# Expert strips issued as one set, and a pair's first output emitted ahead of its second gate product

## The chip, the cores and the metric

The kernel runs on one core of one Trainium2 chip. The metric is the device time of one execution in microseconds (us); the median of several runs is quoted. TensorE is called PE below, VectorE DVE, ScalarE ACT, GpSimd POOL and SyncE SP.

## What is computed

Two transformer blocks run one after the other on 256 tokens of width 1024, in fp32. The first block has two layers, each a token mixer and then a mixture of experts; the second has an attention layer, an RWKV layer and a plain MLP after each. The change touches the mixture of experts alone. Cut to that part, the reference computes, for each of 64 experts `e` and the tokens routed to it (8 experts for each token):

```
def run_block(args):
    e, toks, ws = args
    xb = x_pad[toks]
    hb = jax.nn.silu(xb @ w_gate[e]) * (xb @ w_up[e])
    return (hb @ w_down[e]) * ws[:, None]
...
routed = jax.ops.segment_sum(yb.reshape(P, D), tok_buf, num_segments=T + 1)[:T]
```

`w_gate` and `w_up` are 1024 x 256 for each expert, `w_down` is 256 x 1024. All 64 experts are used in both layers, so a layer loads 64 x 3 MB of expert weights.

## The kernel before, in words

**Groups, pairs, strips.** In `moe` (from L515) the experts are ranked by how many tokens they have, and by rank get room for 128 (4 experts), 64 (28) or 32 tokens (32). 256 such rows make a group, so there are 13 groups in a layer, in the order of `ORDER` (L33). A group is two pairs of 128 rows each (the code's `p_`, 0 and 1; called *units* here). A unit holds `k` experts side by side: 1, 2 or 4, each with a *strip* of 128, 64 or 32 columns of PE's stationary operand, and so of the 128 output partitions. A strip is one matmul of one expert's rows against 512 columns of that expert's weights. Strips of different experts of one unit stand in different column groups of the PE array.

**A unit's steps.** `up` (L842) makes the gate and up products: for each of 8 slices of the contraction, one strip for each expert, into the PSUM tile `gu`. The first four slices read the first half of the experts' weights, the last four the second half, and each half of each expert is a tile of its own. ACT then takes the silu (`hs`, L862), DVE the product (`hm`, L864). `down` (L870) transposes `hm` on PE (`hp`), ACT copies that to `hTe` (L878), and PE makes two outputs of 512 columns (`yps`), each with two slices of the contraction and one strip for each expert; ACT and DVE take them out as a high and a low part (`yH` L887, `yL` L888). `scatter` (L892) adds a group's rows to the tokens (`sca`). `pick` (L798) gathers the tokens of the next group ahead (`gat`, 4 steps of 16 matmuls).

**Loads.** `fetch` (L690) issues a unit's loads on SP: for each expert the first halves (gate and up, 512 KB each, into one 1 MB tile), the second halves, and then `dn` (1 MB): 3, 6 or 12 tiles a unit. All go through one pool of seven 1 MB buffers. A load waits until PE has read the tile that had its buffer.

**Side work.** Between these steps `side_work` (L734, L742) emits pieces of the second block's context path (attention and MLP beside the first mixture, RWKV beside the second), with two weight buffers of their own.

**What sets the order.** The program is traced once; then a scheduler puts each engine's instructions into a fixed order, by the order in which they were written and by when its own model of time finds an instruction's inputs ready. On the chip each engine runs its list in order, and an instruction that waits holds up all behind it. So a strip whose weights are modelled as loaded could be put on PE's list alone, long before the other strips of the same slice: `up` traced the strips one by one, and nothing held them together. `issue_after(x)` puts the instructions traced in its block behind `x` on x's engine.

Of the kernel before, what the change touches and what calls it, by code (L numbers as in the profile page):

```python
# [21 lines left out]
P = 128  # L22
D = 1024
KT = 8
# [14 lines left out]
def dap(ap, off, dims):  # L39
    return bass.AP(tensor=ap.tensor, offset=ap.offset + off, ap=[list(d) for d in dims])  # L40


class Net:
# [471 lines left out]
    def moe(self, l, x, row, mc, mce, rw, rb):  # L515
# [6 lines left out]
        hT = pp.tile([P, KT, S], F32, name="hT")  # L522
# [160 lines left out]
        wk = wks.enter_context(self.pool(name=f"mwk{l}", bufs=2))  # L683
        posT, wHL = self.tables(self.pos, self.wt, NE, mp)
# [5 lines left out]
        def fetch(q, pr):  # L690

            r0, w = groups[q]
            k = P // w
            with tc.issue_after(behind.pop(0)) if len(behind) > 1 else ExitStack():
                rvs = [nc.values_load(self.ei[0:1, r0 + pr * k + u:r0 + pr * k + u + 1],
                                      engines=[mybir.EngineType.SP], min_val=0, max_val=NE - 1) for u in range(k)]
            src = lambda n, u, j: i[n][l, bass.DynSlice(rvs[u], 1)].rearrange("e (p j) f -> p (e j) f", j=j)
            gus = [[self.wtile([2, 4, 256], [((v,), src(n, u, KT)[:, 4 * a:4 * a + 4, :])
                                             for v, n in enumerate(("w_gate", "w_up"))], "gu")
                    for u in range(k)] for a in range(2)]  # L700
            dn = [self.wtile([2, D], [(None, src("w_down", u, 2))], "dn") for u in range(k)]
            behind.append(self.load.ins)
            return gus, dn, False
# [3 lines left out]
        def start(q):  # L707
            r0, w = groups[q]
            sl = slice(r0, r0 + GROUP // w)
            return self.pick(self.pos[:, :, sl], r0, wHL[:, :, sl, :], mce, wk, w)  # L710

        g = drain_last(start(0))
        for q in range(nq):
            bg = BG_GROUP[groups[q][1]]
            if q == nq - 1:
                for t in range(2):
                    r = self.racc[:, t, :]
                    nc.vector.tensor_tensor(r, r, g2, op=OP.mult)
                    r = r.rearrange("q (p j) -> q j p", j=KT)
                    for v in xLH:  # L720
                        nc.vector.scalar_tensor_tensor(r, v[:, t], ALPHA, r, op0=OP.mult, op1=OP.add)
                gb = mp.tile([P, 2, D], F32, tag="xL", name="gb")
                for n, a in enumerate(("ln2_g", "ln2_b")):
                    nc.gpsimd.dma_start(gb[:, n], dap(i[a], l * D, [[0, P], [1, D]]))
            w = [fetch(q, 0)]
            h = [self.up(g, 0, posT, w[0], wk)]
            nxt = start(q + 1) if q + 1 < nq else iter(())
            n = next(nxt, None)
            w.append(fetch(q, 1))
            h.append(self.up(g, 1, posT, w[1], wk))  # L730
            self.down(g, 0, *h[0], w[0][1], wk)
            for _ in range(2):
                next(nxt, None)
            self.side_work(bg / 2)  # L734
            self.down(g, 1, *h[1], w[1][1], wk)
            for _ in nxt:
                pass
            if q < nq - 1:
                self.scatter(g)
            else:  # L740
                self.scatter(g, g2, wk)
            self.side_work(bg / 2)  # L742
            g = n
# [54 lines left out]
    def pick(self, pos, b0, wHL, mce, wk, w=SLOT):  # L798
# [40 lines left out]
        nc.vector.reduce_sum(wsl, wps.rearrange("p a b c -> p a (b c)"), axis=AX.X)  # L839
        yield g  # L840

    def up(self, g, p_, posT, weights, wk, nb=2):  # L842

        nc = self.nc
        gus, dn, wild = weights
        w = g["w"]
        k = P // w
        gu = self.acc([P, 512], "gu")
        sx = lambda j, u: g["xes"][j // 2][:, j % 2, (k * p_ + u) * w:(k * p_ + u + 1) * w]
        for j in range(KT):  # L850
            for v in range(2 if wild else 1):
                for u in range(k):
                    if wild:
                        self.mm(gu[w * u:w * u + w, 256 * v:256 * v + 256], sx(j, u), gus[v][u][:, j, :],
                                j == 0 and v == 0, j == KT - 1)
                    else:
                        self.mm(gu[w * u:w * u + w, :].rearrange("p (a b) -> p a b", a=2), sx(j, u),
                                gus[j // 4][u][:, :, j % 4, :], j == 0, j == KT - 1)
        bp = self.tr([P, S], "bp")
        self.mm(bp, g["eb"][:, P * p_:P * p_ + P], posT, True, True)  # L860
        hs = wk.tile([P, 256], F32, tag="hs", name="hs")
        nc.scalar.activation(hs, gu[:, :256], AF.Silu)  # L862
        hm = wk.tile([P, 2, P], F32, tag="hm", name="hm")
        nc.vector.tensor_tensor(hm.rearrange("q j p -> q p j"), hs.rearrange("q (p j) -> q p j", j=2),  # L864
                                gu[:, 256:].rearrange("q (p j) -> q p j", j=2), op=OP.mult)
        ohT = wk.tile([P, S], F32R, tag="ohT", name="ohT", bufs=nb + 1)
        nc.vector.tensor_scalar(ohT, bp, self.slotp[w], None, op0=OP.is_equal)
        return hm, ohT

    def down(self, g, p_, hm, ohT, dn, wk, nb=2):  # L870

        nc = self.nc
        hp = self.tr([P, 2, P], "hp")
        for j in range(2):
            self.transpose(hp[:, j, :], hm[:, j, :])
        w = g["w"]
        hT = wk.tile([P, 2, P], F32, tag="hT", name="hTe")
        nc.scalar.copy(hT, hp)  # L878
        yH = wk.tile([P, D], F32R, tag="yH", name="yH", bufs=nb)
        yL = wk.tile([P, D], F32R, tag="yL", name="yL", bufs=nb)  # L880
        for hf in range(2):
            sl = slice(hf * 512, hf * 512 + 512)
            y = self.acc([P, 512], "yps")
            for j in range(2):
                for u in range(P // w):
                    self.mm(y[w * u:w * u + w, :], hT[:, j, w * u:w * u + w], dn[u][:, j, sl], j == 0, j == 1)
            nc.scalar.activation(yH[:, sl], y, AF.Copy, scale=g["wsl"][:, p_:p_ + 1])  # L887
            nc.vector.scalar_tensor_tensor(yL[:, sl], y, g["wsl"][:, p_:p_ + 1], yH[:, sl], op0=OP.mult,  # L888
                                           op1=OP.subtract)
        g["ys"].append((ohT, yH, yL))  # L890
# [931 lines left out]
def drain_last(gen):  # L1822
    for v in gen:
        pass
    return v
# [114 lines left out]
```

## Time and profile before

| | |
|---|---|
| median of 3 runs | 3206.11 us (3203.72 to 3206.66) |
| the profiled execution's own time | 3199.65 us |
| its span, first to last instruction | 3197.9 us |
| granted TensorE clock, mean over the span | 0.925 of full speed |
| PE / DVE / ACT / POOL busy | 89% / 53% / 38% / 14% |
| mean over the span, moved by DMA | 234 GB/s |

The mixture of experts runs from about 350 to 1135 us (layer 0) and from about 1455 to 2135 us (layer 1) of the span: 1465 us in all. An fp32 matmul stands in the trace as two records, so a strip is "x2"; the trace shows 2048 records of `gu` and 1024 of `yps`, that is 1024 and 512 strips. Busy time is the time in which at least one record of a group runs, so strips that run side by side count once.

### The profile page before, as it was taken

How to read it: one execution, taken by the hardware profiler on the slowest of the kernel's cores; microseconds unless marked ns; L12 is line 12 of the kernel's file. 1: busy time of each engine (PE TensorE's matmuls, PEld its weight loads, DVE VectorE, ACT ScalarE, POOL GpSimd, SP SyncE). 2: the span in 40 equal slices, each digit the busy share in tenths (PEclk: the TensorE clock that was granted, in tenths of full speed). 3: DMA queues.
4: the chain of work that ended last, by engine and by line, in shares of the span. 5: the costliest groups of instructions: out<-in, count | busy, mean ns of one | idle time of the engine just before them, and what ended most of it. 6: DMA issues, size and time to landing. Idle time of an engine off the chain costs nothing.

```text
span 3197.9 us, 52845 instructions
## 1 busy us (share of the span) xinstructions
PE 2857.3 (89%) x20518; PEld 1879.6 (59%) x20518; DVE 1703.9 (53%) x3348; ACT 1224.0 (38%) x2237; POOL 450.4 (14%) x653
## 2 busy tenths in 40 slices
PE   5998988978999999999888989779999997878899
PEld 2776533544565568785444434345678785656698
DVE  3556433433344466663433434258876775565576
ACT  2553333322223246531323223224554445454443
POOL 1102000000000000100010010003023204343032
PEclk9999988989999999999999999889999997567899
DMA  9764798999988787636888888875345541002552
GB/s 334 280 220 161 268 349 316 347 355 349 401 299 323 257 298 269 218 125 248 313 323 306 336 320 321 320 264 181 104 126 172 171 129 25 11 8 67 176 189 80
DMA packets 237407, 748.25 MB, mean 234 GB/s; under 512 B 24288, under 2 KB 39560, under 8 KB 208480
## 3 DMA queue, kind: packets, MB, share of 16 engines
q1 hardware_dynamic: 230896, 728.56, 63.0%
q0 software_dynamic: 5920, 15.19, 1.6%
q8 instruction: 165, 2.70, 0.3%
q10 hardware_dynamic: 336, 1.06, 0.1%
q14 instruction: 90, 0.74, 0.1%
HBM read 738.56 MB, written 6.18 MB: 233 GB/s over the span
## 4 chain that ended last, share of the span: by engine, by line
PE 67%; DVE 9%; DMA 5%; ACT 5%; issue 3%; SPq 1%; POOL 0%; DVEq 0%; ACTq 0%; POOLq 0%
PE gu L76 12%; PE mu L76 9%; PE yps L76 7%; PE w L76 7%; PE gat L76 3%; PE sca L76 3%; DMA gu<-in_w_up_dram 2%; PE rk L76 2%; PE pg L76 2%; PE adaps L76 2%; DVE wl L240 1%; DMA w<-in_mlp_w_dram 1%; PE ao L76 1%; PE zy L76 1%; PE rv L76 1%
## 5 line engine op out<-in xcount | busy, mean ns | idle before, releaser
L240 DVE TENSOR_TENSOR wl<-w,wh 128x1024 fp32r<-128x1024 f32 (+1 forms) x432 | 472.9, 1101 | 322.1 <-ACT wh L239 308.7
L239 ACT CAST wh<-w 128x1024 fp32r<-128x1024 f32 (+1 forms) x432 | 377.7, 882 | 574.2 <-PE mu L76 159.9
L76 PE MATMUL gu<-gu,xe 128*32 128x512 f32 (+2 forms) x2048 | 502.3, 627 | 29.4 <-DMA gu<-in_w_up_dram 29.4
L76 PEld LDWEIGHTS gu<-gu,xe 128*32 128x32 f32 (+2 forms) x2048 | 134.2, 130 | 268.3 <-issue 242.7
L76 PE MATMUL yps<-dn,hTe 128*32 128x512 f32 (+2 forms) x1024 | 258.6, 654 | 3.2 <-ACT hTe L878 2.3
L76 PE MATMUL mu<-hTH,wh 128*128 128x256 f32 x768 | 218.3, 289 | 0.8 <-ACT wh L239 0.5
L76 PE MATMUL mu<-hTL,wh 128*128 128x256 f32 x768 | 215.9, 285 | 0.0
L76 PE MATMUL mu<-hTH,wl 128*128 128x256 f32 x768 | 208.8, 287 | 0.1
L888 DVE SCALAR_TENSOR_TENSOR yL<-yps,wsl,yH 128x512 fp32r<-128x512 f32 x104 | 78.0, 750 | 186.3 <-ACT yH L887 186.2
L76 PEld LDWEIGHTS mu<-hTH,wh 128*128 128x128 f32 x768 | 148.0, 193 | 19.7 <-issue 12.4
L76 PE MATMUL w<-wl,aTH 128*128 128x512 f32 x384 | 153.7, 400 | 1.3 <-DVE wl L240 1.2
L76 PEld LDWEIGHTS yps<-dn,hTe 128*32 128x32 f32 (+2 forms) x1024 | 73.7, 134 | 135.9 <-issue 122.9
L76 PE MATMUL w<-wh,aTH 128*128 128x512 f32 x384 | 139.2, 404 | 14.6 <-ACT wh L239 12.3
L76 PE MATMUL w<-wh,aTL 128*128 128x512 f32 x384 | 152.1, 396 | 0.2 <-DVE aTL L240 0.2
L76 PEld LDWEIGHTS mu<-hTL,wh 128*128 128x128 f32 x768 | 148.1, 193 | 4.7 <-issue 3.3
L76 PEld LDWEIGHTS mu<-hTH,wl 128*128 128x128 f32 x768 | 143.1, 193 | 11.2 <-issue 5.0
L76 PE MATMUL adaps<-adaw,lhs 128*32 128x512 f32 x768 | 125.9, 668 | 26.3 <-DMA adaw<-in_ada_w_dram 14.0
L887 ACT ACTIVATE yH<-yps,wsl 128x512 fp32r<-128x512 f32 x104 | 71.5, 687 | 184.8 <-PE yps L76 180.6
L1080 POOL TENSOR_TENSOR x<-x,opt 128x512 f32<-128x512 f32 x56 | 97.8, 1767 | 250.3 <-DVE opt L1079 250.3
L864 DVE TENSOR_TENSOR hm<-hs,gu 128x256 f32<-128x256 f32 x52 | 31.6, 607 | 174.2 <-ACT hs L862 174.1
L807 POOL CAST eb<-ident 128x256 fp32r<-128x256 f32 x26 | 13.7, 530 | 773.5 <-PE bp L76 629.9
L824 DVE TENSOR_SCALAR xe<-gat,mce 128x256 f32<-128x256 f32 x104 | 56.3, 541 | 110.4 <-ACT xe L822 109.8
(609 smaller groups left out, 6124.3 us busy)
## 6 DMA issues: line engine op xcount, KB each, us to landing
gu<-in_w_gate_dram SPq DMA_DIRECT2D x256, 512.0 KB, 8.2
gu<-in_w_up_dram SPq DMA_DIRECT2D x256, 512.0 KB, 9.8
dn<-in_w_down_dram SPq DMA_DIRECT2D x128, 1024.0 KB, 10.5
w<-in_mlp_w_dram SPq DMA_DIRECT2D x96, 1024.0 KB, 6.3
adaw<-in_w_ada_dram SPq DMA_DIRECT2D x48, 1024.0 KB, 8.0
adaw<-in_ada_w_dram SPq DMA_DIRECT2D x48, 1024.0 KB, 6.0
w<-in_w_in_dram SPq DMA_DIRECT2D x30, 1024.0 KB, 6.4
w<-in_rwkv_w_rkv_dram SPq DMA_DIRECT2D x20, 1024.0 KB, 4.9
```

The costliest lines, as they stand in the source:

```text
L76: return self.nc.tensor.matmul(out, lhsT, rhs, start=start, stop=stop, skip_group_check=True)
L239: self.nc.scalar.copy(h, f)
L240: self.nc.vector.tensor_tensor(l, f, h, op=OP.subtract)
L807: nc.gpsimd.tensor_copy(eb, self.ident[:, b0:b0 + nblk].unsqueeze(2).to_broadcast([P, nblk, w]))
L824: nc.vector.tensor_scalar(xe[:, 1, :], ps[:, 1, :], mce[:, 1, 2 * jj + 1:2 * jj + 2], mce[:, 0, 2 * jj + 1:2 * jj + 2], op0=OP.mult, op1=O ...
L864: nc.vector.tensor_tensor(hm.rearrange("q j p -> q p j"), hs.rearrange("q (p j) -> q p j", j=2), gu[:, 256:].rearrange("q (p j) -> q p j", ...
L887: nc.scalar.activation(yH[:, sl], y, AF.Copy, scale=g["wsl"][:, p_:p_ + 1])
L888: nc.vector.scalar_tensor_tensor(yL[:, sl], y, g["wsl"][:, p_:p_ + 1], yH[:, sl], op0=OP.mult, op1=OP.subtract)
L1080: (self.nc.vector if last else self.nc.gpsimd).tensor_tensor(x[:, t, sl], x[:, t, sl], tt, op=OP.add)
```

## The change

Two edits. First, a helper `strips` is added. Where a unit's strips first read a set of weight tiles (slices 0 and 4 of `up`, slice 0 of the first output of `down`), it traces the last expert's strip first and puts the other experts' strips behind it on PE; the loads are issued in the experts' order, so the last expert's weights come last. The 128-row units (one expert) are left as they were, and so is the overflow path (`wild`), which the profile shows not taken. Second, in the loop over groups the first unit's `down` is traced ahead of the second unit's `up`, behind two of the four gather steps of the next group; the second unit's `down` comes behind the other two. No instruction of the kernel is added or taken away.

```
@@ -727,14 +727,14 @@
             w.append(fetch(q, 1))
-            h.append(self.up(g, 1, posT, w[1], wk))
-            self.down(g, 0, *h[0], w[0][1], wk)
             for _ in range(2):
                 next(nxt, None)
+            self.down(g, 0, *h[0], w[0][1], wk)
+            h.append(self.up(g, 1, posT, w[1], wk))
             self.side_work(bg / 2)
-            self.down(g, 1, *h[1], w[1][1], wk)
             for _ in nxt:
                 pass
+            self.down(g, 1, *h[1], w[1][1], wk)
...
+    def strips(self, k, strip, first):
+
+        if first and k > 1:
+            with self.tc.issue_after(strip(k - 1).ins):
+                for u in range(k - 1):
+                    strip(u)
+        else:
+            for u in range(k):
+                strip(u)
+
...
         for j in range(KT):
             for v in range(2 if wild else 1):
-                for u in range(k):
+                def strip(u):
...
+                self.strips(k, strip, j % 4 == 0 and not wild)
...
             for j in range(2):
-                for u in range(P // w):
-                    self.mm(y[w * u:w * u + w, :], hT[:, j, w * u:w * u + w], dn[u][:, j, sl], j == 0, j == 1)
+                self.strips(P // w, lambda u: self.mm(y[w * u:w * u + w, :], hT[:, j, w * u:w * u + w],
+                                                      dn[u][:, j, sl], j == 0, j == 1), hf == 0 and j == 0)
```

What stands in an engine's list is shown at three places, all on PE in layer 0. `atp`, `asps`, `aops`, `adaps` and `adat` are side work (attention and modulation of the context path).

The first place is the second unit of the first group of 32-row experts, second half of its gate and up weights. Before:

```order
L76 MATMUL gu<-gu,xe 32x512 x2
L80 MATMUL atp<-ident,ap 128x128 x4
L76 MATMUL asps<-kT,qT 128x256 x2
L76 MATMUL gu<-gu,xe 32x512
L80 MATMUL atp<-ident,ap 128x128 x4
L76 MATMUL aops<-apT,v 64x256 x4
L80 MATMUL adat<-ident,adab 128x128 x4
L76 MATMUL asps<-kT,qT 128x256 x2
L76 MATMUL gu<-gu,xe 32x512 x13
```

and now:

```order
L76 MATMUL asps<-kT,qT 128x256 x2
L80 MATMUL atp<-ident,ap 128x128 x4
L76 MATMUL aops<-apT,v 64x256 x4
L80 MATMUL adat<-ident,adab 128x128 x4
L76 MATMUL asps<-kT,qT 128x256 x2
L76 MATMUL gu<-gu,xe 32x512 x16
L80 MATMUL atp<-ident,ap 128x128 x4
```

The three strips that stood alone, or two together, ahead of the thirteen now stand with them; the side work that stood between is ahead of all sixteen.

The second place is the same unit's output. Before:

```order
L76 MATMUL yps<-dn,hTe 32x512 x2
L76 MATMUL bp<-posT,eb 128x256
L80 MATMUL atp<-ident,ap 128x128 x4
L76 MATMUL sca<-yH,ohT 128x512
L76 MATMUL sca<-yL,ohT 128x512
L76 MATMUL aops<-apT,v 64x256 x4
L76 MATMUL asps<-kT,qT 128x256
L76 MATMUL yps<-dn,hTe 32x512 x10
```

and now:

```order
L80 MATMUL hp<-ident,hm 128x128 x2
L76 MATMUL bp<-posT,eb 128x256
L76 MATMUL asps<-kT,qT 128x256 x2
L80 MATMUL atp<-ident,ap 128x128 x4
L76 MATMUL aops<-apT,v 64x256 x4
L76 MATMUL asps<-kT,qT 128x256
L76 MATMUL yps<-dn,hTe 32x512 x16
```

Six strips (of the first three experts) stood ahead of the ten, in two pieces of which the second is shown; now all sixteen stand together.

The third place is the first group of 64-row experts, where the first unit's output meets the second unit's gate product. Before:

```order
L76 MATMUL gu<-gu,xe 64x512 x16
L80 MATMUL atp<-ident,ap 128x128 x4
L76 MATMUL asps<-kT,qT 128x256
L80 MATMUL hp<-ident,hm 128x128 x2
L76 MATMUL asps<-kT,qT 128x256
L76 MATMUL gu<-gu,xe 64x512
L76 MATMUL yps<-dn,hTe 64x512 x8
```

and now:

```order
L80 MATMUL atp<-ident,ap 128x128 x4
L80 MATMUL hp<-ident,hm 128x128 x2
L76 MATMUL bp<-posT,eb 128x256
L76 MATMUL aops<-apT,v 64x256 x4
L80 MATMUL adat<-ident,adab 128x128 x4
L76 MATMUL yps<-dn,hTe 64x512 x8
L76 MATMUL wps<-wHL,oh 128x8 x4
L76 MATMUL adaps<-adaw,lhs_117 32x512 x8
L76 MATMUL asps<-kT,qT 128x256
L76 MATMUL gu<-gu,xe 64x512 x8
```

The second unit's first `gu` strip, alone ahead of the output before, now stands behind it, with its set; two gather steps stand ahead of the rows shown. (`wps` are small matmuls of `pick`, `bp` one of `up`.)

## Rows read from the trace of the kernel before

**Rows 1.** The page: span, busy time, the costliest groups of strips, the chain.

```profile
span 3197.9 us, 52845 instructions
...
PE 2857.3 (89%) x20518; PEld 1879.6 (59%) x20518; DVE 1703.9 (53%) x3348; ACT 1224.0 (38%) x2237; POOL 450.4 (14%) x653
...
PE 67%; DVE 9%; DMA 5%; ACT 5%; issue 3%; SPq 1%; POOL 0%; DVEq 0%; ACTq 0%; POOLq 0%
...
L76 PE MATMUL gu<-gu,xe 128*32 128x512 f32 (+2 forms) x2048 | 502.3, 627 | 29.4 <-DMA gu<-in_w_up_dram 29.4
...
L76 PE MATMUL yps<-dn,hTe 128*32 128x512 f32 (+2 forms) x1024 | 258.6, 654 | 3.2 <-ACT hTe L878 2.3
```

**Rows 2.** Busy time by stretch, both mixtures; last: clock, DMA share, GB/s.

```profile
350.00:1135.00 785.00, 729.01 (x3703) 388.94 (x3704) 323.36 (x641) 238.45 (x468) 26.72 (x38) 0.96 0.89 334
1455.00:2135.00 680.00, 604.04 (x4654) 294.29 (x4653) 257.04 (x561) 187.50 (x376) 58.83 (x137) 0.93 0.83 309
```

**Rows 3.** What PE waited for, layer 0, then layer 1: us, times, longest.

```profile
PE gu L76 <- DMA gu<-in_w_up_dram: 13.2, 5, 6.0
PE w L76 <- ACT wh L239: 12.3, 3, 7.0
...
PE hp L80 <- DVE hm L864: 3.5, 4, 1.1
...
PE gu L76 <- DMA gu<-in_w_up_dram: 16.1, 14, 2.7
...
PE hp L80 <- DVE hm L864: 8.9, 13, 1.2
...
PE yps L76 <- ACT hTe L878: 2.0, 5, 0.8
```

**Rows 4.** Timeline of PE, layer 0: a lone strip among full-width matmuls (start, us).

```profile
706.70 0.28 PE L76 MATMUL mu<-hTL,wh 128*128 128x256 f32 x1
706.82 0.28 PE L76 MATMUL mu<-hTH,wl 128*128 128x256 f32 x1
707.03 1.07 PE L76 MATMUL gu<-gu,xe 128*64 128x512 f32 x2
708.03 0.39 PE L76 MATMUL mu<-hTL,wh 128*128 128x256 f32 x1
708.25 0.28 PE L76 MATMUL mu<-hTH,wl 128*128 128x256 f32 x1
708.37 0.28 PE L76 MATMUL mu<-hTH,wh 128*128 128x256 f32 x1
```

**Rows 5.** Timeline of PE: whole sets and sets without their first strips.

```profile
449.30 3.62 PE L76 MATMUL gu<-gu,xe 128*32 128x512 f32 x26
...
590.61 3.65 PE L76 MATMUL gu<-gu,xe 128*64 128x512 f32 x16
...
596.16 3.65 PE L76 MATMUL gu<-gu,xe 128*64 128x512 f32 x14
```

**Rows 6.** What bounded SP's queue, layer 1: the issue of loads waits for PE.

```profile
SPq L102 <- PE yps L76: 197.0, 25, 21.2
SPq L102 <- PE gu L76: 196.0, 46, 16.5
```

**Rows 7.** DMA totals of layer 0, then of layer 1.

```profile
DMA packets 67380, 262.37 MB, mean 334 GB/s; under 512 B 6368, under 2 KB 6368, under 8 KB 56440
...
DMA packets 50603, 209.96 MB, mean 309 GB/s; under 512 B 5600, under 2 KB 7152, under 8 KB 42350
```

**Rows 8.** Two stretches of layer 0 with the loads at their fastest.

```profile
590.00:606.00 16.00, 16.00 (x80) 8.57 (x80) 5.81 (x11) 4.68 (x9) 0.00 (x0) 1.00 1.02 408
1040.00:1056.00 16.00, 16.00 (x88) 8.99 (x86) 4.94 (x8) 3.13 (x6) 0.00 (x0) 1.00 1.03 410
```

**Rows 9.** A set that waited for weights, layer 1, and its transposes.

```profile
2048.68 6.35 PE L76 MATMUL gu<-gu,xe 128*32 128x512 f32 x26 [2.36 <-DMA gu<-in_w_up_dram]
2056.14 0.44 PE L80 MATMUL hp<-ident,hm 128*128 128x128 f32 x2 [1.11 <-DVE hm L864]
```

**Rows 10.** The first microseconds of that set: clock 0.50.

```profile
2048.70:2052.00 3.30, 3.30 (x16) 0.77 (x20) 0.00 (x0) 0.00 (x0) 0.00 (x0) 0.50 1.02 414
```

**Rows 11.** The steps between a gate product and its output (ns: min, median, max).

```profile
L862 ACT ACTIVATE hs<-gu x52: 383/383/385, 365.9 to 2122.7; 128x256 f32<-128x256 f32 x52
L864 DVE TENSOR_TENSOR hm<-hs,gu x52: 578/604/634, 367.0 to 2123.1; 128x256 f32<-128x256 f32 x52
...
L878 ACT COPY hTe<-hp x52: 361/372/385, 370.3 to 2127.7; 128x256 f32<-128x256 f32 x52
```

More of the change, by code (lines that the diff above doesn't have):

```diff
@@ L851, in up @@
             for v in range(2 if wild else 1):
-                for u in range(k):
+                def strip(u):
                     if wild:
[L854 to L858, printed above, removed]
+                        return self.mm(gu[w * u:w * u + w, 256 * v:256 * v + 256], sx(j, u), gus[v][u][:, j, :],
+                                       j == 0 and v == 0, j == KT - 1)
+                    return self.mm(gu[w * u:w * u + w, :].rearrange("p (a b) -> p a b", a=2), sx(j, u),
+                                   gus[j // 4][u][:, :, j % 4, :], j == 0, j == KT - 1)
+                self.strips(k, strip, j % 4 == 0 and not wild)
         bp = self.tr([P, S], "bp")
```

## The prediction

> **What bounds the kernel now.** I read the page first: PE is busy for 89% of the span and holds 67% of the chain that ended last, and the two costliest groups of strips are `gu` (502.3 us) and `yps` (258.6 us) [rows 1]. All of these lie in the two mixtures of experts, so the next view is busy time by stretch [rows 2]. There the reader sees two loads of nearly the same weight. In layer 0 PE is busy for 729.0 of 785 us, and the DMA engines for 0.89 of it, 699 us; in layer 1 it is 604.0 of 680 us against 0.83, 564 us. PE leads in both, but only by 4 and 7%. The waits of PE [rows 3] show little: it stood still for expert weights for 13.2 us (5 times) and 16.1 us (14 times). SP on the other hand waits mostly for PE: 393 us of layer 1 went by while the next load's buffer was still to be read by a `yps` or a `gu` strip [rows 6]. So the loads follow PE, and what PE loses on its list is lost in the end, as long as the loads can keep up.
>
> **The first edit, on PE.** What does a strip cost alone? Four slices of a 64-row unit with all 8 strips ("x16") take 3.65 us; four slices with only 7 ("x14"), because one strip was issued earlier, take 3.65 us as well, and 13 strips of a 32-row unit ("x26"), where a full set has 16, take 3.62 [rows 5]. A slice takes about 0.89 us (a quarter of that, less the tail of the last) however many of its strips are there; the strips of a slice run side by side, and one that stood alone earlier is a slice paid twice. On top comes the change from full-width work to a strip and back. Around a lone strip the full-width `mu` records go from one start every 0.12 us to 706.82, 708.03, 708.25 [rows 4]: from the one at 706.82 to the one at 708.25 it is 1.43 us, where 0.24 would do. A lone strip costs PE 1.19 us, 0.89 for the slice and 0.30 for the two changes.
>
> How many are there? I counted in PE's list. Strips that stand next to each other and in different columns share a slice; each piece of strips between other work is counted for itself. Before, the 1536 strips make 755 slices (384 in layer 0, 371 in layer 1) in 226 pieces (120 and 106). Now they make 624, the fewest there can be (52 units of 8 and 4), in 143 pieces (72 and 71). So 131 slices and 83 pieces go:
>
> - layer 0: 72 x 0.89 + 48 x 0.30 = 78 us of PE
> - layer 1: 59 x 0.89 + 35 x 0.30 = 63 us of PE
>
> Together 141 us, and that is the upper bound of the gain. The lower bound of this term is nothing: a lone strip that ran while the next expert's weights were still on their way was free, and with it gone PE just waits. At most 19 waits for weights stand in the trace [rows 3], so at most 19 lone strips, 23 us, are surely of that kind as the kernel stands; but waits will grow, since the loads now are the greater of the two.
>
> **How much of it stays.** With 78 and 63 us less, PE has 651 us of work in layer 0 against 699 of DMA, and 541 against 564 in layer 1. The loads lead, by 7 and 4%: the picture of before with the parts changed. Before, the stretch was longer than its busier part by 785 / 729.0 = 1.077 and by 680 / 604.0 = 1.126 [rows 2]. I take the same factors on the new busier part: 699 x 1.077 = 753 us, and 564 x 1.126 = 635 us. That is 32 and 45 us less, **77 us** in all, a little over half of what PE is freed of. The ends I keep are 0 and 141.
>
> Can the loads run that fast? Layer 0 would move its 262.37 MB in 753 us, 348 GB/s against 334 now, layer 1 its 209.96 MB in 635 us, 331 against 309 [rows 7]. In two stretches of 16 us they ran at 408 and 410 GB/s [rows 8], so yes. The Trainium skill speaks against this: "DMA: Bandwidth & Descriptors", in the section "Where 436 GB/s comes from", says that for transfers from HBM the HBM side binds at about 358 GB/s for a core. By it layer 0 has 733 us of loads and layer 1 586 us, and with the same factors the gain would be nothing in layer 0 and 20 us in layer 1. The two stretches above contradict that figure, and I go by them; that the loads set the pace at a lower rate is my first rival.
>
> **The second edit.** It moves the first unit's transposes and output ahead of the second unit's gate product, and the last two gather steps ahead of the second output. Nothing is added. What it changes is the cover of one chain: from a unit's last `gu` strip through `hs` (0.383 us) and `hm` (0.604 us) to `hp`, and from `hp` through `hTe` (0.372 us) to `yps` [rows 11]. Before, the second unit's strips often stood in the first gap; now a gather step (8 matmuls, some 0.95 us at 0.12) or side work does. PE waited 12.4 us in all for `hm` and some 2 for `hTe` before [rows 3], 1.2 us at the worst. If every one of the 52 units had that worst case with only one gather step over it, 52 x (1.2 - 0.95) = 13 us come on top; if the cover is the better one, up to 12 us go. I take 0, since every unit still has a gather step or side work there. The four buffers of `dn` of a 32-row unit are read before the second unit's `gu` set instead of after its first strips, which lets the loads behind them start earlier; I count that in the factor above.
>
> **Queues.** On SP the 640 loads of weights in the expert pool stand in the same order as before; 39 of 367 other loads move, most to 4 to 12 expert loads later, with the side work they belong to. PE waited 12.3 us for such weights in layer 0 [rows 3]; doubled, that is 12 us, and it is in the range. POOL, ACT and DVE have the same instructions. Behind a set that waits stand gathers and side work that could have run; that is the price in the second rival.
>
> **The sum.** The profiled execution took 3199.65 us; less 77 is 3122.7. It lay 6.5 us under the median of the runs shown, so the median I expect is **3129 us**. About 0.2% (6.4 us) is what a measurement of this kernel can tell from no change.
>
> **The rivals.**
>
> *The loads set the pace already (3186).* The lone strips were put where weights were missing, and if the loads cannot go faster, most of the strips only fill a wait. For it: SP waits for PE in turn [rows 6], seven buffers hold barely a set of four and the next three, so a load leaves late whatever PE does in between. Against: 83 pieces and only 19 waits. If the loads go on at their shares of now, layer 0 gains nothing, and layer 1 goes only as far as layer 0's rate of 334 GB/s, 629 us, if at all; I put this case at 0 to 40 us, 20 in the middle, so 3186. Chance 0.23, of which 0.05 lies within 0.2%.
>
> *All of it stays (3068).* The loads keep up and PE stays the bound: 78 + 63 = 141 us less, 3065 to 3070. For it: the rate of 410 GB/s was reached with PE busy throughout [rows 8]. Against: PE and DMA are too near each other. Chance 0.10.
>
> *Slower: a set waits for its last weights, and the clock falls (3289).* The price of a bad wait is in the trace: a set of 13 strips waited 2.36 us, and then took 6.35 us where others take 3.62 [rows 5, 9], since the granted clock was 0.50, the 1.2 GHz level, when it began [rows 10]. That is 5.1 us. The 64- and 32-row units number 44 (22 in each layer); one such wait in each is 224 us, and against 141 freed the kernel would be 83 us slower, 3289. It decides from 141 / 44 = 3.2 us of new waiting in a unit on. The Trainium skill has the rule for this: "TensorE: Matmul & The Clock Gate", section "Loop structure matters more than you think", calls a wait for a load ahead of each matmul the bad form of loop, because PE runs cold after it. By the rule the strips that filled such waits kept PE warm; the one set above agrees about the clock, but it was split and fell all the same. Chance 0.07.
>
> *It doesn't do what it says.* PE's list shows the sets whole, so this is only left as strips of a set that do not run side by side; the sets of rows 5 do. No chance of its own.
>
> **How the numbers follow.** My forecast, 40 to 110 us gained (3096 to 3166), has 0.60; the pace of the loads 0.23; all of it 0.10; slower 0.07. The range reaches from a gain of 126 us to one of 16 us, 3080 to 3190: it leaves out most of the slower case, the poorer part of the first rival and the better part of the full gain, some 0.2. Faster by over 0.2% is 0.60 + 0.18 + 0.10 = 0.88, within 0.2% is 0.05, slower 0.07.
>
> **What would show it.** In the changed kernel's profile `gu` and `yps` together should be busy for some 600 to 640 us instead of 761, with no `gu` record "x2" between other work. PE's busy time in the two mixtures should fall by over 100 us, and the DMA share rise to about 0.92 in layer 0 and 0.89 in layer 1. PE's waits for `gu` weights should rise from 29 us to some 60 to 100. The forecast is wrong if those waits pass 140 us or the mean clock of the mixtures falls under 0.90 (the slower case), or if the mixtures keep 785 and 680 us though the strips are whole (the loads' pace).

## The result and the profile after

The changed kernel takes **3167.41 us** in the median of 4 runs (3152.20 to 3171.01), the kernel before 3206.07 beside it: ratio 0.9885, interval 0.9862 to 0.9909, or 38.7 us less. The forecast was 3129 us, 77 us less: the direction held, half of the size did not. The profiled execution took 3164.82 us, with a span of 3163.0.

The page of the changed kernel; it answers to [rows 1]:

```profile
span 3163.0 us, 52849 instructions
...
PE 2778.4 (88%) x20518; PEld 1890.2 (60%) x20518; DVE 1710.5 (54%) x3348; ACT 1220.3 (39%) x2236; POOL 454.0 (14%) x653
...
L76 PE MATMUL gu<-gu,xe 128*32 128x512 f32 (+2 forms) x2048 | 408.1, 656 | 31.9 <-DMA gu<-in_w_up_dram 31.9
...
L76 PE MATMUL yps<-dn,hTe 128*32 128x512 f32 (+2 forms) x1024 | 214.4, 678 | 15.8 <-DMA dn<-in_w_down_dram 6.8
```

`gu` and `yps` together fell from 760.9 to 622.5 us, 138 less. That is close to the 141 us priced, but not the same thing: before, a `gu` piece and a `yps` piece often ran side by side, and such time stands in both sums. The time in which a strip of either kind ran fell from 729.7 to 622.0 us, 108 less, and PE's whole busy time by 78.9. To see what took the rest, I cut both traces at the same events: first `gu` strip and last `sca` matmul of each layer. Busy time by stretch, of before (layer 0's mixture, between, layer 1's mixture, behind it):

```profile
359.00:1126.00 767.00, 713.67 (x3590) 377.06 (x3589) 308.88 (x614) 233.85 (x460) 21.94 (x31) 0.96 0.89 335
1126.00:1472.00 346.00, 330.64 (x1984) 255.95 (x1983) 217.81 (x437) 150.50 (x238) 31.65 (x47) 0.98 0.64 223
1472.00:2135.00 663.00, 587.34 (x4585) 284.44 (x4584) 251.84 (x550) 184.08 (x370) 57.63 (x135) 0.93 0.84 311
2135.00:3198.00 1063.00, 926.20 (x8589) 747.36 (x8587) 734.36 (x1359) 503.67 (x929) 288.48 (x357) 0.87 0.35 116
```

and of the changed kernel:

```profile
361.00:1081.00 720.00, 654.52 (x3613) 373.97 (x3612) 311.45 (x617) 234.36 (x463) 19.88 (x31) 0.94 0.94 361
1081.00:1428.00 347.00, 323.92 (x1922) 250.83 (x1922) 215.97 (x429) 147.21 (x234) 34.77 (x47) 0.95 0.60 211
1428.00:2091.00 663.00, 576.91 (x4626) 303.32 (x4625) 257.61 (x556) 184.73 (x374) 58.04 (x135) 0.90 0.86 318
2091.00:3163.00 1072.00, 919.60 (x8589) 743.85 (x8587) 735.06 (x1359) 502.38 (x927) 290.52 (x357) 0.87 0.34 111
```

Layer 0 is 48 us shorter (forecast 32), layer 1 not at all (forecast 45), and the part behind it, which holds no strips, 9 us longer. In layer 1 the strips are whole and PE is busy for only 10 us less; its granted clock, a mean over the levels 1.2 and 2.4 GHz, fell from 0.93 to 0.90.

The stretches do not hold the same side work. `rv`, the value products of RWKV, has 64 records in this part of the run. Its busy time between the layers and in layer 1 (columns: PE, PEld, ACT), before and then in the changed kernel; one record lies across the border before:

```profile
1126.00:1472.00 346.00, 18.50 (x42) 7.67 (x42) 1.16 (x2) 0.98 0.64 223
1472.00:2135.00 663.00, 10.56 (x23) 4.10 (x22) 1.17 (x2) 0.93 0.84 311
...
1081.00:1428.00 347.00, 0.00 (x0) 0.00 (x0) 0.00 (x0) 0.95 0.60 211
1428.00:2091.00 663.00, 28.44 (x64) 11.86 (x64) 2.35 (x4) 0.90 0.86 318
```

The scheduler put 42 of them, 18 us of PE, into the first two groups of layer 1, and the stretch that they left is no shorter. So "layer 1 gained nothing" compares a layer with 18 us more work in it; the runs below have to be read with this in mind.

PE's waits in layer 1 (1455:2095), to set beside the second half of [rows 3]: us, times, longest.

```profile
PE gu L76 <- DMA gu<-in_w_up_dram: 21.7, 7, 5.8
PE rtk L80 <- DVE BK L1477: 14.9, 5, 3.9
PE hp L80 <- DVE hm L874: 10.8, 11, 2.9
PE rcum L76 <- DVE sg L1447: 6.3, 3, 2.4
```

Weights are waited for little more than before (21.7 us against 16.1); beside them stand waits of the RWKV side work (`rtk`, `rcum`) and of the transposes `hp` for `hm`, up to 2.9 us where 1.2 was the longest. I held three theories: **L**, the loads through seven buffers set layer 1's pace; **C**, the freed PE time comes back as work at the lower clock; **S**, the side work in layer 1 sets it.

### The profile page after: what moved, and what is told of

It is laid out like the page before. It is cut to its first block, busy times and chain, and to the rows that moved or that the text cites. A ratio compares the mean times of both kernels' runs of the same rounds, so it can differ in the third digit from the quotient of the medians.

```text
span 3163.0 us, 52849 instructions
## 1 busy us (share of the span) xinstructions
PE 2778.4 (88%) x20518; PEld 1890.2 (60%) x20518; DVE 1710.5 (54%) x3348; ACT 1220.3 (39%) x2236; POOL 454.0 (14%) x653
## 4 chain that ended last, share of the span: by engine, by line
PE 37%; DVE 8%; ACT 4%; DMA 3%; issue 2%; POOL 0%; SPq 0%; DVEq 0%; ACTq 0%; POOLq 0%
PE mu L76 6%; PE gu L76 5%; PE w L76 4%; PE yps L76 3%; PE rv L76 2%; PE rk L76 1%; PE sca L76 1%; PE gat L76 1%; DMA gu<-in_w_up_dram 1%; PE rsc L76 1%; DVE wl L240 1%; PE zy L76 1%; PE su L76 1%; PE r1t L76 1%; PE ro L76 1%
## 5 line engine op out<-in xcount | busy, mean ns | idle before, releaser
L76 PE MATMUL gu<-gu,xe 128*32 128x512 f32 (+2 forms) x2048 | 408.1, 656 | 31.9 <-DMA gu<-in_w_up_dram 31.9
L76 PEld LDWEIGHTS gu<-gu,xe 128*32 128x32 f32 (+2 forms) x2048 | 141.2, 136 | 238.4 <-issue 215.5
L76 PE MATMUL yps<-dn,hTe 128*32 128x512 f32 (+2 forms) x1024 | 214.4, 678 | 15.8 <-DMA dn<-in_w_down_dram 6.8
L76 PEld LDWEIGHTS yps<-dn,hTe 128*32 128x32 f32 (+2 forms) x1024 | 60.8, 139 | 134.1 <-issue 117.6
L822 ACT ACTIVATE xe<-gat,mce 128x256 f32<-128x256 f32 x104 | 58.7, 564 | 160.3 <-PE gu L76 135.9
```

The source lines that it names most:

```text
L76: return self.nc.tensor.matmul(out, lhsT, rhs, start=start, stop=stop, skip_group_check=True)
L822: nc.scalar.activation(xe[:, 0, :], ps[:, 0, :], AF.Identity, scale=mce[:, 1, 2 * jj:2 * jj + 1], bias=mce[:, 0, 2 * jj:2 * jj + 1])
```

## The experiments

Each ratio is to the kernel before in runs on the same chip (its medians there: 3197.38, 3202.32, 3202.10 and 3200.47 us for the four groups that follow). Stretches are cut as above.

**First group: the second edit alone, and the number of weight buffers.**

`order_only`: the kernel before with the new order of emission, strips as they were.

```
-            h.append(self.up(g, 1, posT, w[1], wk))
-            self.down(g, 0, *h[0], w[0][1], wk)
             for _ in range(2):
                 next(nxt, None)
+            self.down(g, 0, *h[0], w[0][1], wk)
+            h.append(self.up(g, 1, posT, w[1], wk))
             self.side_work(bg / 2)
-            self.down(g, 1, *h[1], w[1][1], wk)
             for _ in nxt:
                 pass
+            self.down(g, 1, *h[1], w[1][1], wk)
```

> The second edit alone: first output ahead of the second gate product, strips still issued one by one. If the gain of 39 us came from the strips alone, the time is that of before, 3200 to 3212 us, and layer 0 keeps about 767 us from its first gu strip to its last scatter. If the new order by itself lets the loads leave earlier, layer 0 falls by 10 us or more, to 3180 to 3196. Layer 1 (662 us before and 663 after the change) stays at 660 to 666 by both.

Measured 3212.33 us, ratio 1.004 (1.0028 to 1.0052): slightly slower. Layer 0 768.1 us, layer 1 675.5 (662.9 before), where both expectations had 660 to 666. The second edit is not free. Part of it is again side work: 48 `rv` records stand in layer 1 here, 22 before.

`slim7`, the control for the next: the changed kernel with five small tiles kept once instead of twice.

```
-        oh = wk.tile([P, 2, nblk, w], F32R, tag="oh", name="oh")
+        oh = wk.tile([P, 2, nblk, w], F32R, tag="oh", name="oh", bufs=1)
...
```

> Control for the next run: the changed kernel with five small working tiles (oh, hs, hm, hT, wm) in one buffer instead of two, still seven weight buffers. All theories: within 10 us of the changed kernel's 3167, as these tiles are read shortly after they are written.

Measured 3172.28 us, 0.9926 (0.9909 to 0.9943): 5 us above the changed kernel's median and, by the two ratios to the kernel before, 13. So the small tiles cost little, if anything. Layers 723.4 and 657.9 us.

`slim8`: the same with an eighth weight buffer.

```
-            with net.weights(f"we{l}", 7):
+            with net.weights(f"we{l}", 8):
```

> The same with eight weight buffers. Theory L (loads): in layer 1 what sets the pace is that a set of four strips holds four of seven buffers until its last slice, so that the next loads leave late; with eight, a whole next set can be under way. Then the 32-row groups of layer 1 fall from 78 us towards 65, layer 1 by some 45 us, and the time to about 3120. Theory S (side work): the RWKV pieces' chains of small steps set layer 1's pace; then nothing changes, 3157 to 3177. Theory C (clock): freed PE waits and falls to the lower level, so the rest costs more; then the time falls only as far as the mean clock of layer 1 rises from 0.90.

Measured 3149.16 us, 0.9852 (0.9836 to 0.9869). Layers 682.4 and 635.8 us, but 1120.9 behind them. Busy time by stretch, layer 0, layer 1 and behind:

```profile
361.00:1043.00 682.00, 613.79 (x3380) 339.15 (x3379) 280.88 (x574) 214.02 (x430) 17.62 (x28) 0.94 0.95 370
1388.00:2024.00 636.00, 570.13 (x4173) 303.22 (x4172) 253.62 (x534) 177.69 (x350) 46.07 (x108) 0.94 0.91 346
2024.00:3145.00 1121.00, 948.86 (x9226) 769.47 (x9224) 761.90 (x1429) 530.12 (x978) 306.21 (x388) 0.85 0.32 108
```

Layer 1 lost 453 matmul records, and 637 more stand behind it: side work slid out. So its 28 us are no clean evidence for L. The total lies between what L and S named. C is not set aside by it either, since the granted clock of layer 1 rose from 0.90 to 0.94 as the time fell.

`buf6`: the changed kernel with six buffers.

> The changed kernel with six weight buffers. Theory L: each of the six sets of a 32-row group waits for one more load, some 2.6 us (1 MB at about 400 GB/s), 16 us a group and some 125 us over the eight groups of both layers: 3270 to 3310. Theory S: under 20 us slower, since the loads are not what is waited for. Theory C: slower, with a clock in the mixtures under 0.88.

Measured 3236.55 us, 1.0128 (1.0107 to 1.0149): the sets with six buffers are slower than the kernel before. In layer 1 PE waits 42.1 us for `gu` weights and 23.9 for `dn`. The time is 69 us above the changed kernel, too little for L and too much for S; C's clock under 0.88 is seen in layer 1 (0.87) and not in layer 0 (0.95). The buffers count, as L says; that they are what holds layer 1 at seven is not shown by it.

**Second group: the side work, and each layer's sets alone.**

`noside1`: no RWKV pieces between the units of layer 1; they run behind the mixture.

```
-            bg = BG_GROUP[groups[q][1]]
+            bg = BG_GROUP[groups[q][1]] if l == 0 else 0
```

> The changed kernel without the RWKV pieces between the units of layer 1's mixture; all of them run behind it. Layer 1's stretch from the first gate product to the last scatter was 663.4 us in the changed kernel, DMA 0.86 busy at 318 GB/s. Theory L (the seven weight buffers and their loads set the pace): only the side work's own loads go, so the stretch stays at 630 us or more, with DMA still below 0.90. Theory S (the chains of the RWKV side work on PE and VectorE set the pace of layer 1): the stretch falls by 60 us or more, to 600 us or less, with DMA above 0.92. Theory C (the freed PE time is paid back by the lower clock level): PE is busy some 150 us less and its granted clock falls below 0.87, and the stretch lies between the two. The total is longer under each, by 60 to 250 us, as the moved work then has nothing to hide behind.

Measured 3411.22 us, 1.0655 (1.0636 to 1.0675). Layer 1's stretch, and PE's waits in it:

```profile
1372.00:1952.00 580.00, 448.37 (x2254) 225.83 (x2253) 146.44 (x246) 84.24 (x156) 7.78 (x17) 0.89 0.93 352
```

```profile
PE gu L76 <- DMA gu<-in_w_up_dram: 67.2, 13, 7.8
PE yps L76 <- DMA dn<-in_w_down_dram: 28.0, 8, 5.2
PE hp L80 <- DVE hm L874: 27.3, 23, 4.4
```

663.7 became 579.7 us, with DMA at 0.93: what S expected, and L's 630 is missed by 50. Only now does PE wait for weights as I had thought the changed kernel would (95 us with `dn`). C missed on the clock, 0.89 instead of below 0.87. With side work in it, layer 1 is not at the pace of its loads; without it, it nearly is. PE's busy time in the layer fell by 129 us with the pieces (576.9 to 448.4), so whether they cost by their chains of small steps, as S has it, or by PE's time is not separated.

`setsl0` and `setsl1`: sets in one layer only, new order in both.

```
+        self.sets = l == 0
...
-        if first and k > 1:
+        if first and k > 1 and self.sets:
```

> Sets in layer 0 alone, with the new order of emission in both layers. If the gain lies in layer 0 alone (theories L and C as the two profiles read): layer 0 takes 715 to 725 us, layer 1 660 to 677, and the total is 3155 to 3172 us, no slower than the whole change, so the sets of layer 1 are worth nothing or cost a few us. If layer 1's sets do help and their gain is only hidden by side work that came into it: layer 1 is over 680 us and the total over 3180.

Measured 3167.25 us, 0.9886 (0.9867 to 0.9906): as fast as the whole change. Layers 722.8 and 674.7 us. Layer 1 holds the same work as in the changed kernel (4626 matmul records in both), so there its sets take 11 us off the stretch (674.7 to 663.7); the part behind it is 8 us longer in the changed kernel, and of the total nothing is left.

> Sets in layer 1 alone, new order of emission in both. If the sets are worth nothing in layer 1 (L, C): layer 0 at 765 to 770 us as with the new order alone, layer 1 at 655 to 675, total 3200 to 3220 us. If they are worth something there and only lost it to layer 0's change: layer 1 below 645 and the total below 3190.

Measured 3194.20 us, 0.9973 (0.9960 to 0.9987); layers 768.4 and 646.4 us. Layer 1's sets do shorten it, by 29 us against the new order alone (675.5). The two hold the same `rv` records, 48, so this is like against like; layer 1 of `order_only`, then of `setsl1`:

```profile
1477.00:2153.00 676.00, 616.43 (x4612) 288.12 (x4610) 253.60 (x548) 184.63 (x374) 57.47 (x135) 0.97 0.84 309
...
1476.00:2122.00 646.00, 561.09 (x4602) 294.41 (x4601) 252.43 (x543) 182.65 (x368) 54.87 (x129) 0.91 0.88 323
```

The time lies just outside what either expectation named. With sets in both layers this gain seems to vanish; the next groups of runs look for where.

`slim8_o`: eight buffers, and larger budgets of side work in layer 1.

```
+            bg = (BG_GROUP if l == 0 else {128: 0, 64: 22, 32: 66})[groups[q][1]]
```

> The changed kernel with eight weight buffers as in the run before, and larger budgets of side work in layer 1 (22 and 66 us instead of 12 and 40 per group), which bring back into the mixture some of the RWKV pieces that had slid behind it. Theory L: layer 1 has time on PE beside its loads, so its stretch of 635.5 us grows by less than 15 while the part behind the mixture falls from 1121 to below 1095: total 3115 to 3140 us. Theory S: the pieces lengthen the mixture by what they shorten the part behind it: layer 1 at 650 to 670, total 3140 to 3155 us.

Measured 3184.61 us, 0.9941 (0.9924 to 0.9957). Both theories miss: layer 1 went to 670.9 us and the part behind it did not shrink (1134.2). The first half speaks for S: with eight buffers and the side work back, layer 1 is no shorter than with seven. Why the rest stayed long I did not follow up.

**Third group: where the second edit costs.** The 13 groups of a layer have strips of one width each; the first and the last have 128 rows. The expectations from here on call such a group of two units a unit. The time from one group's last `sca` to the next one's (from the first `gu` in each layer), summed by width, us:

| groups | layer 0 before | changed | old128 | layer 1 before | changed | old128 |
|---|---|---|---|---|---|---|
| first, 128 rows | 34 | 36 | 34 | 44 | 50 | 46 |
| seven of 64 rows | 337 | 303 | 303 | 286 | 268 | 256 |
| four of 32 rows | 363 | 339 | 342 | 307 | 311 | 306 |
| last, 128 rows | 34 | 41 | 31 | 27 | 35 | 27 |

The groups of 128 rows have one strip per slice: the sets change nothing in them, and yet they got longer. PE's timeline over the last group of layer 1 in the changed kernel:

```profile
2056.82 7.13 PE L76 MATMUL gu<-gu,xe 128*128 128x512 f32 x16
2063.88 0.33 PE L76 MATMUL su<-RA,TK 128*64 128x64 f32 x2
2064.14 0.45 PE L76 MATMUL sa<-Zs,T 64*64 64x64 f32 x8
2064.52 0.45 PE L76 MATMUL su<-RA,TK 128*64 128x64 f32 x6
2067.89 0.69 PE L80 MATMUL hp<-ident,hm 128*128 128x128 f32 x2 [2.92 <-DVE hm L874]
2068.22 0.56 PE L76 MATMUL bp<-posT,eb 128*128 128x256 f32 x1
2068.71 0.70 PE L76 MATMUL su<-RA,TK 128*64 128x64 f32 x8
2069.34 5.98 PE L76 MATMUL yps<-dn,hTe 128*128 128x512 f32 x8
2075.16 7.03 PE L76 MATMUL gu<-gu,xe 128*128 128x512 f32 x16
2083.30 0.44 PE L80 MATMUL hp<-ident,hm 128*128 128x128 f32 x2 [1.11 <-DVE hm L874]
2084.20 3.70 PE L76 MATMUL yps<-dn,hTe 128*128 128x512 f32 x8 [0.46 <-ACT hTe L888]
```

The chain from `gu` over `hm` and `hTe` to `yps` lies bare: no next group to gather for, no budget of side work (0 for this width), and the second gate product now stands behind the first output. Leftovers of side work fall into the gap, PE stands for 2.9 us, and the `yps` behind it takes 5.98 us at a granted clock of 0.61 where the later one takes 3.70 at 1.00. The chain alone costs the 1.11 and 0.46 us of the second pass; in the first, DVE was still at three instructions of 2.0 us each (L721) and a copy, and began `hm` at 2067.25, 3.3 us after the last strip.

`old128`: the changed kernel with the order of before in the four groups of 128 rows alone.

```
+            old = groups[q][1] in (128,)
+            if old:
+                h.append(self.up(g, 1, posT, w[1], wk))
+                self.down(g, 0, *h[0], w[0][1], wk)
             for _ in range(2):
                 next(nxt, None)
-            self.down(g, 0, *h[0], w[0][1], wk)
-            h.append(self.up(g, 1, posT, w[1], wk))
+            if not old:
+                self.down(g, 0, *h[0], w[0][1], wk)
+                h.append(self.up(g, 1, posT, w[1], wk))
...
```

> The changed kernel with the order of emission of before (second gate product ahead of the first output) in the four units of 128-row strips alone. Those four units took 24 us more with the new order, with and without sets (layer 0: first +2, last +7; layer 1: first +6, last +8). Theory E (with nothing else for PE between a gate product and its own output, the chain gate product, ACT, DVE, transposes, ACT, output lies bare): the total falls by 15 to 25 us against the changed kernel's 3167.4, to 3142 to 3152 us, and the last unit of layer 1 is back at some 27 us. Theory F (the longer units only took in side work that must be done anyway): the total stays within 7 us of the changed kernel's, as the side work moves elsewhere.

Measured **3126.80 us**, 0.9759 (0.9730 to 0.9788): 75 us under the kernel before, 41 under the changed one. The same group, and the stretches of both layers and behind:

```profile
2038.33 13.89 PE L76 MATMUL gu<-gu,xe 128*128 128x512 f32 x32
2052.06 0.38 PE L80 MATMUL hp<-ident,hm 128*128 128x128 f32 x2
2052.96 3.70 PE L76 MATMUL yps<-dn,hTe 128*128 128x512 f32 x8 [0.52 <-ACT hTe L896]
2056.50 0.38 PE L80 MATMUL hp<-ident,hm 128*128 128x128 f32 x2
2057.70 3.70 PE L76 MATMUL yps<-dn,hTe 128*128 128x512 f32 x8 [0.82 <-ACT hTe L896]
```

```profile
358.00:1068.00 710.00, 647.53 (x3578) 365.61 (x3578) 307.85 (x613) 231.83 (x459) 19.82 (x31) 0.94 0.95 361
1430.00:2065.00 635.00, 551.62 (x4585) 292.24 (x4583) 252.90 (x550) 182.90 (x370) 57.84 (x135) 0.91 0.87 325
2065.00:3126.00 1061.00, 923.39 (x8587) 747.35 (x8586) 737.93 (x1358) 503.19 (x929) 288.60 (x357) 0.86 0.34 116
```

E has the direction and misses the size (3142 to 3152). By the table the four groups give back about 25 us. Of these, PE's idle time is 4 us (8.6 to 4.7 in the four groups) and the groups' own steps 5 (116.3 to 111.2); the other 16 are side work that no longer runs in them (37.1 to 21.0 us of PE), which is what F had in mind. The rest comes with where side work then stands. Layer 1's other groups are 17 us shorter and the stretch between the layers 15 longer (362.1 us): the 42 `rv` records stand between the layers again. The part behind layer 1 is 10 us shorter. The spans differ by 37 us in all. That the edit costs 41 us beside the sets is measured; that the bare chains cost it is shown for 9 us at most.

`old128_64`: the old order in the 64-row groups too (`in (128, 64)`).

> The same for the units of 64-row strips too, so that the new order stands in the 32-row units alone and the sets everywhere. With the new order alone the 64-row units took 12 us more in layer 1 and 8 us less in layer 0 than before. Theory E (a bare chain costs wherever PE has nothing beside it): 64-row units of layer 1 fall by some 10 us and those of layer 0 rise by as much or less, total within 10 us of the run with the four 128-row units alone. If the sets need the new order in 64-row units too (tiles held by a whole set while the first output's weights wait): layer 1's 64-row units rise above 40 us each and the total is above 3160 us.

Measured 3169.26 us, 0.9904 (0.9874 to 0.9933), 42 us above `old128`. The total is what the last sentence expected if the sets need the new order here; the 64-row groups of layer 1 take 38 to 47 us (over 40 each was expected), the layer 654.3, the part behind it 1081.2. But all 64 `rv` records stand in layer 1 again, so not all of the 42 us is the order's.

`slim8v128`: eight buffers with the old order in the 128-row groups; the gated product is written over its first factor, which frees a tile.

> Eight weight buffers (room made by single small tiles and by writing the gated product over its first factor) together with the old order in the 128-row units. Eight buffers alone gave 3149.2 us. Theory E: another 15 to 25 us less, 3124 to 3134 us. Theory F: 3142 to 3156 us.

Measured 3125.21 us, 0.9757 (0.9727 to 0.9787). Layers 672.6 (at 374 GB/s) and 623.4 us, 1120.2 behind; layer 0:

```profile
360.00:1033.00 673.00, 613.71 (x3371) 340.29 (x3370) 278.44 (x574) 217.20 (x431) 17.58 (x28) 0.94 0.97 374
```

The total is theory E's number, but no better than seven buffers, as side work slid out again.

`slim8v128_64`: the same with the old order in the 64-row groups too.

> The same with eight buffers and the old order in 64- and 128-row units. With an eighth buffer a 64-row unit has room for its whole set beside the waiting output weights, so by theory E the total is within 10 us of the run with the 128-row units alone; if it is over 15 us more, the old order holds loads back even with eight buffers.

Measured 3133.19 us, 0.9782 (0.9754 to 0.9811): within 10 us of the last one, as expected; with eight buffers the 64-row groups can stand either order.

**Fourth group: the sets alone, with the 128-row groups in the old order.** `nosets128` takes the sets out of `old128`; `o128sl0` and `o128sl1` keep them in one layer.

> No sets at all; new order of emission in the 32- and 64-row units, old order in the four 128-row units. If the sets alone carry the gain of the run with sets and the old order in 128-row units (3126.8 us): 3195 to 3210 us, as before (3202 to 3206). If the new order of the narrow units earns part of it: 3170 to 3195 us.

Measured 3226.94 us (3215.91 to 3230.41), 1.0088 (1.0054 to 1.0123). Both expectations were too low: without sets the new order in the narrow groups costs some 26 us against the kernel before (16 by the profiled executions, 3214.1 against 3197.9 us of span). Without sets it splits more slices: the time in which a strip of either kind ran is 761.7 us, 729.7 before. Layers 764.9 and 673.7 us:

```profile
361.00:1126.00 765.00, 724.45 (x3586) 373.07 (x3585) 306.91 (x613) 232.93 (x460) 19.62 (x31) 0.98 0.90 336
1469.00:2143.00 674.00, 622.14 (x4629) 292.62 (x4627) 255.69 (x556) 178.78 (x368) 57.89 (x135) 0.98 0.84 310
```

> Old order in the 128-row units, sets in layer 0 alone. If layer 0's sets earn what its stretch shows (709 against 767 us, less the 16 us that slid behind it): 3160 to 3172 us with layer 1 at 655 to 670 us. If the two layers' gains are not additive: below 3150 or above 3180.

Measured 3155.36 us, 0.9854 (0.9811 to 0.9898). Layers 710.9 and 659.0 us.

> Old order in the 128-row units, sets in layer 1 alone. If layer 1's sets are worth what its stretch shows with the old order there (635 against 663 us): 3165 to 3182 us with layer 0 at 760 to 768. If they are worth nothing, as the changed kernel's 663.7 us seemed to say: 3195 us or more.

Measured 3189.97 us, 0.9968 (0.9951 to 0.9985). Layers 760.8 and 652.7 us. In both runs the time lies between the two expectations named: more gain in layer 0 and less in layer 1 than the stretches had promised.

Medians of the eight corners, us. They come from five sets of runs, in which the kernel before had medians from 3197 to 3206 us, so differences under 10 us say little:

| order in 128-row groups | no sets | layer 0 | layer 1 | both |
|---|---|---|---|---|
| new | 3212.3 | 3167.3 | 3194.2 | 3167.4 |
| old | 3226.9 | 3155.4 | 3190.0 | 3126.8 |

With the old order in the wide groups the sets earn 72 us in layer 0, 37 in layer 1 and 100 in both, nearly a sum. With the new order there they earn 45, 18 and 45. So with sets in layer 0, those of layer 1 add to the run only where the wide groups keep the old order. Undoing the second edit in these four groups helps with both sets (41 us); without any, the medians are 15 us longer, though the profiled spans are 3 us shorter (3217.0 and 3214.1). The cost is not fixed. That it depends on where the scheduler puts the side work fits the `rv` records, but no run here holds the side work in place, so it is not shown.

## Why the forecast was half right

- **Slices and pieces (first edit on PE): the price of a slice held, the 141 us on PE did not come.** 131 slices were priced at 117 us and 83 pieces at 25; the time in which a strip ran fell by 108. PE's busy time in the two mixtures fell by 70 (59 and 10), where I had asked for over 100. In layer 1 strips ran 40 us less (366 to 326) and `rv` 18 us more. The strips' mean granted clock there fell from 0.93 to 0.88; their time multiplied by it fell by 55 us, so by this estimate 15 us came back through the clock. The 100 us that the sets earn with the order held cannot be set beside the bound of 141, since that base, `nosets128`, has more split slices than the kernel before.
- **"I take 0, since every unit still has a gather step or side work there" (second edit): the step that failed.** The last group of each layer has no next group to gather for, and all four groups of 128 rows have a budget of side work of 0, both to be read in the code. Beside the sets, the new order in these four groups cost 41 us (`old128`), about as much as the forecast fell short (38). My upper end of 13 us priced a chain's wait and nothing else. The wait was the smaller part: some 9 us in these groups, with 16 of side work that came into them, and the rest outside them. What the term left out is that a new order moves the side work; which move costs what stays open. In the narrow groups the new order is still needed beside the sets with seven buffers, as far as `old128_64` shows it.
- **How much stays: layer 0 better, layer 1 worse.** In layer 0 the shares came as forecast: DMA 0.94, PE's lower at 0.91, 719.4 us. That the loads set its pace is not shown, as PE waited only 13.5 us for expert weights in it (10.2 for `gu`, 3.3 for `dn`). The rate of 361 GB/s, and 374 in `slim8v128` over 673 us, answers the rule of the Trainium skill ("DMA: Bandwidth & Descriptors", "Where 436 GB/s comes from", about 358 GB/s for a core from HBM, half of what a stack gives): the trace of this one core goes above it, by 1 and 4%. In layer 1 I took DMA as the busier part and forecast 45 us less; it became 0, with DMA at 0.86 and PE at 0.87, and 28 less in `old128`. `noside1` shows what was left out: the side work, which I had put into no term, keeps layer 1 some 84 us above what it takes without it.
- **Waits for weights:** forecast 60 to 100 us for `gu`, measured 31.9. The sign that the loads lead did not come. The 12.3 us of [rows 3] that I read as waits for the side work's weights are waits for ACT's copy `wh`; that a load stood behind them is not shown.
- **Luck:** the median of `old128`, 3126.8 us, lies 2 us from my 3129, but not by my sum: its layer 0 is 58 us shorter (forecast 32), its layer 1 28 (45), and the stretch between them 16 longer (0).
- **The clock (the rival "slower"): the mechanism is real, the price is not.** In the new order the mean granted clock of layer 1 is 0.97 to 0.98 without sets and 0.91 with them (`order_only`, `nosets128`; `setsl1`, `o128sl1`); in the kernel before, without sets, it is 0.93. Two sets of layer 1 in the changed kernel show what it does to one set, with granted clocks of 1.00 and 0.63 over them; ahead of the second, PE stood three times for 0.5 to 1.0 us:

```profile
1783.41 3.64 PE L76 MATMUL gu<-gu,xe 128*32 128x512 f32 x32
...
1820.29 6.02 PE L76 MATMUL gu<-gu,xe 128*32 128x512 f32 x32 [0.97 <-DMA gu<-in_w_up_dram]
```

  So in the new order the lone strips went with the higher level, as the rule of the Trainium skill named beside that rival would have it ("TensorE: Matmul & The Clock Gate", "Loop structure matters more than you think"). But with the same side work in it, layer 1 is 29 us shorter at the lower clock (`setsl1` against `order_only`) and 21 (`o128sl1` against `nosets128`): the strips saved outweigh the clock. The slower case did not come.
- **"The loads set the pace already" (first rival)** named SP's waits for PE. They stayed: in layer 1 (1427.5:2091) they read

```profile
SPq L102 <- PE gu L76: 240.5, 43, 18.2
SPq L102 <- PE yps L76: 138.3, 23, 13.6
```

  379 us against 393 [rows 6], now more of it on `gu`, since a set holds all its tiles until its last slice. Its time, 3186, was 19 us too high and so nearer than mine, but by luck: it had layer 0 gain nothing and layer 1 up to 40 us, and the reverse was measured.

What stays open: which single wait of the side work binds layer 1, and why the part behind the mixture shifts by up to 20 us between kernels that differ only in the mixture (1062 to 1081 us with seven buffers). The first edit alone, with the old order everywhere, was not tried: in the 32-row groups four `dn` and four `gu` tiles at once don't fit in seven buffers. With eight they would, and that run is missing. The best versions run are `old128` and `slim8v128`, equal within their spread, 2.4% under the kernel before.

## What to carry to other kernels

When an edit reorders a loop, price it for every kind of iteration, those at the ends too, which have no neighbour and no filler to cover a chain. Before two stretches are compared, count whether they still hold the same work: here 18 us of it moved across the border. The busy times of two groups of instructions don't add up where they ran side by side. Packing strips into full slices pays by the slices it removes, as far as the loads and the side work woven into the loop let it; take the side work out once to learn which of the two sets the pace. A gain that appears with either of two edits but not with both is a sign to run the missing corner before believing in a limit.

## What was not expected of the hardware

- Layer 1 ran faster with PE's granted clock at 0.91 than at 0.97 (646 against 676 us, `setsl1` and `order_only`): a high clock here went with slices paid twice.
- The DMA engines were 0.95 busy at 361 GB/s and 0.97 at 374 over whole mixtures, while stretches of 16 us in the kernel before reach 410 at a share of 1.03 [rows 8]: from 0.95 to 1.03 the share grows by 8% and the rate by 14%, so the share is no straight measure of the rate.
